# The first chunk of a streaming-encoder trunk, contraction block by contraction block: both token tiles with each block of weights, loads in that order

## The chip, the core and the metric

One NeuronCore of a Trainium2 chip runs the whole program. The metric is the device time of one execution in microseconds (us). The engines are PE (matrix multiply), ACT (activation), DVE (vector), POOL and SP; SP issues nearly all loads here, and every engine works through its own queue in the order in which the program was laid out.

## What is computed

Two layers on x of 256 tokens by 1024 features. Each layer is a half-step feed-forward block, a mixer (differential attention beside an mLSTM) and a second half-step feed-forward block, each between RMS norms:

```python
def _swiglu(h, w_in, w_out):
    gate, up = jnp.split(h @ w_in, 2, axis=-1)
    return (jax.nn.silu(gate) * up) @ w_out

for l in range(DEPTH):
    g = norm_gains[l]
    h = _swiglu(_rmsnorm(x, g[0]), ffn_w_in[l, 0], ffn_w_out[l, 0])
    x = x + 0.5 * _rmsnorm(h, g[1])
    ...
```

Only the first feed-forward block of the first layer matters here: h @ w_in for the first 256 of 2816 hidden columns (its "chunk 0"), and what comes right behind it. The contraction runs over 1024 features, in 8 blocks of 128.

## The kernel before

All large operands are split into a high and a low part, so one product of a token block with a weight block is three matmuls of 512 columns on PE: high x high, low x high, high x low. Weights come in "pieces" of 1 MB (128 x 2048), each with four contraction blocks of 512 columns (256 gate, 256 up) in the input product. A piece is loaded by SP into one of three buffers `wr`; ACT makes its high part `wh` (a cast), DVE its low part `wl` (a subtraction, the split), for the whole pieces in two halves of 1024 columns (lines 287, 288). A buffer is free for the load of the third piece behind it when DVE has split its second half. SP issues loads in order and waits for that.

The first two pieces are handled by hand (`first_chunk`, line 332). They are loaded block by block, and the table `FIRST` lists every step, in an order that all three engines keep:

- `T t hf k`: PE transposes block k of half hf of token tile t of x into a PSUM bank (line 348)
- `A`, `B` (same indices): ACT and DVE make the high and the low part of it, scaled by the gain (lines 354, 357), both into the tile `both`
- `H i k`, `L i k`: cast (ACT, 366) and split (DVE, 370) of block k of piece i
- `M t i k`: the three matmuls of tile t with block k of piece i into the tile's bank `pins[t]` (376 to 378)
- `W n`, `V n`: n filler matmuls of 512 and 128 columns on constants (`warm`, line 389), while PE has nothing to do

`start` (line 303) issues the loads of x, of the two hand-made pieces and, through `constants`, of the identity and gains `c`. Tile 0's x comes in quarters of 256 columns for the first half, otherwise in halves of 512.

What follows the first chunk is laid out by a scheduler from its own estimate of times: four squares for the norm, two for each token tile (line 438, on ACT), the input products of chunk 1 (lines 400 to 402 into `pin`, with the first two whole pieces), the hidden values h of chunk 0 (`sil` on ACT, line 265; `h` on DVE), their transposes on PE, `hh` and `hl` from these (ACT line 545, DVE line 546), and then chunk 0's output product into four banks `bk`, with `hh`, `hl` and the third whole piece. The pieces of chunk 2, the fourth and fifth, are cast and split in between. In the names of the rows `wr`, `wh`, `wl` are the pieces' tiles, c and x the constants and x, `ptr`, `pin` and `bk` PSUM banks.

Of the kernel before, what the change touches and what calls it, by code (L numbers as in the profile page):

```python
# [24 lines left out]
P = 128  # L25
# [11 lines left out]
TURN = 2  # L37
AHEAD = 2
AT = (0, 2, 6, 6, 7, 22, 24, 24, 24, 24, 36, 40, 24, 46, 34, 50, 43, 52, 52, 57, 61, 60, 61, 67, 67, 69, 71, 78, 74, 74, 78, 84)
FIRST = """W6 V3 T000 T001 A000 A001 B000 B001 W1 V1 T002 T003 H00 L00 A002 A003 B002 B003 W1 V1 M000 H01 L01  # L40
    T100 T101 T102 T103 M001 H02 L02 A100 A101 B100 B101 A102 A103 B102 B103 M002 H03 L03
    T010 T011 T012 T013 M100 A010 A011 B010 B011 A012 A013 B012 B013 T110 T111 T112 T113 M101 M102 M003 M103
    H10 L10 A110 A111 B110 B111 H11 L11 A112 A113 B112 B113 M010 M110 M011 M111 H12 L12 M012 M112 H13 L13 M013 M113"""
SCRATCH = 1024
FILL = 896
# [85 lines left out]
class _Trunk:  # L131
# [173 lines left out]
    def start(self):  # L305

        nc, a = self.nc, self.a
        sp, act = nc.sync, nc.scalar

        def load_x(q, t, hf, c=slice(0, 512)):  # L310
            q.dma_start(self.x[t][:, hf * 512 + c.start:hf * 512 + c.stop], a["x"][t, hf][:, c])

        def load_w(q, i, k, n=1):
            if k == 0:
                self.early[i] = self.raw_tile(i)
            q.dma_start(self.early[i].rearrange("p a b -> p (a b)")[:, k * 512:(k + n) * 512].rearrange("p (k c) -> p k c", k=n),
                        a["w"][i].rearrange("a b -> (a b)").rearrange("(k p c) -> p k c", k=4, p=P)[:, k:k + n])

        self.constants()
        load_x(sp, 0, 0, slice(0, 256))  # L320
        load_x(sp, 0, 0, slice(256, 512))
        load_w(act, 0, 0)
        load_w(sp, 0, 1)
        load_x(sp, 1, 0)
        load_w(sp, 0, 2)
        load_w(sp, 0, 3)
        load_x(sp, 0, 1)
        load_x(sp, 1, 1)
        load_w(sp, 1, 0, 2)
        load_w(sp, 1, 2, 2)  # L330

    def first_chunk(self, pins, xT):


        nc = self.nc
        ptr, th, tl, hi, lo = {}, {}, {}, {}, {}

        def T(t, hf, k):

            if k % 2 == 0:  # L340
                bank = (self.bank_pin if hf else self.bank_bk)((P, 4, P)) if k else self.bank_tr((P, 4, P))
                for j in range(k, k + 2):
                    ptr[t, hf, j] = bank[:, j, :]
            if k == 0:
                th[t, hf], tl[t, hf] = self.operand(hf, t, t == 0)
                xT[t].append((th[t, hf], tl[t, hf]))
            at = (4 * hf + k) * P
            nc.tensor.transpose(ptr[t, hf, k], self.x[t][:, at:at + P], self.ident)

        def gain(hf, k):  # L350
            return self.gpre[:, 4 * hf + k:4 * hf + k + 1]

        def A(t, hf, k):
            nc.scalar.activation(th[t, hf][:, k], ptr[t, hf, k], AF.Copy, scale=gain(hf, k))

        def B(t, hf, k):
            nc.vector.scalar_tensor_tensor(tl[t, hf][:, k], ptr[t, hf, k], gain(hf, k), th[t, hf][:, k].bitcast(F32),
                                           op0=ALU.mult, op1=ALU.subtract)

        def raw(i, k):  # L360
            return self.early[i].rearrange("p a b -> p (a b)")[:, k * 512:(k + 1) * 512]

        def H(i, k):
            if k % 2 == 0:
                lo[i, k // 2], hi[i, k // 2] = self.half_tiles(i, k // 2)
            self.cast = nc.scalar.activation(self.cols({k // 2: (hi[i, k // 2], lo[i, k // 2])}, k)[0], raw(i, k), AF.Copy)

        def L(i, k):
            wh, wl = self.cols({k // 2: (hi[i, k // 2], lo[i, k // 2])}, k)
            self.split = nc.vector.tensor_tensor(wl, raw(i, k), wh.bitcast(F32), op=ALU.subtract)  # L370

        def M(t, i, k):
            wh, wl = self.cols({k // 2: (hi[i, k // 2], lo[i, k // 2])}, k)
            xh, xl = th[t, i][:, k], tl[t, i][:, k]
            start, stop = (i, k) == (0, 0), (i, k) == (1, 3)
            nc.tensor.matmul(pins[t], xh, wh, start=start, stop=False)
            nc.tensor.matmul(pins[t], xl, wh, start=False, stop=False)
            nc.tensor.matmul(pins[t], xh, wl, start=False, stop=stop)  # L378

        ops = dict(T=T, A=A, B=B, H=H, L=L, M=M, W=self.warm, V=lambda n: self.warm(n, P))  # L380
        for step in FIRST.split():
            ops[step[0]](*(int(c) for c in step[1:]))

    def warm(self, n, cols=512):

        bank = self.bank_bk()
        one = self.nc.const_aps.tensor(1.0, (P, 1), mybir.dt.bfloat16)
        for _ in range(n):
            self.nc.tensor.matmul(bank[:, 0:cols], one.broadcast_to([P, P]), one.broadcast_to([P, cols]), start=True, stop=True)

    @staticmethod
    def cols(piece, k):
# [5 lines left out]
    def mm3(self, ps, xh, xl, wh, wl, start, stop):  # L398
        mm = self.nc.tensor.matmul
        mm(ps, xh, wh, start=start, stop=False)  # L400
        mm(ps, xh, wl, start=False, stop=False)  # L401
        mm(ps, xl, wh, start=False, stop=stop)  # L402
# [852 lines left out]
```

## Time and profile before

| | us |
|---|---|
| median of 3 runs | 977.52 |
| lowest, highest | 977.37, 977.88 |
| the profiled execution | 978.05 |
| its span | 976.3 |
| PE busy | 968.3 |
| DVE busy | 710.5 |
| ACT busy | 567.5 |

The profile is one execution; its times count from the span's start. A matmul's end is modelled, so PE's work is best read from the starts of its instructions. The rows of a timeline give start, duration, engine, line, output and inputs, and how often a row repeats; in brackets how long the engine was idle ahead of it and what it waited for. A DMA's row on SP or ACT (SPq, ACTq) is its issue; when its data landed stands in the view of the DMA issues.

### The profile page before, as it was taken

To read this page: it belongs to the slowest core of one execution; us is meant where nothing else is said; L and a number is where in the kernel's file an instruction comes from. 1 tells how busy PE (TensorE), PEld (TensorE's weight loads), DVE (VectorE), ACT (ScalarE), POOL (GpSimd) and SP (SyncE) were. 2 spreads that over 40 slices of the span, in tenths; PEclk is the share of its full clock that TensorE was granted. 3 is DMA by queue.
4 is the path that set the end of the run, shared out by engine and by line. 5 is a ranking of instruction groups with operands and counts; after the bars stand their busy time and mean duration, and the time that the engine had idled before them with its cause. 6 is when DMAs were issued, how large, how long until landed. Compare 5 with 4: busy or idle time off the path is not lost.

```text
span 976.3 us, 13528 instructions
## 1 busy us (share of the span) xinstructions
PE 968.3 (99%) x5067; PEld 817.2 (84%) x5067; DVE 710.5 (73%) x1177; ACT 567.5 (58%) x1041; POOL 29.0 (3%) x55
## 2 busy tenths in 40 slices
PE   9999999999999999999999999999999999999997
PEld 6888888888788888888888888888888888888886
DVE  6787676689867677667687767676997687776764
ACT  7665555477856565455475545454778475555541
POOL 2000000000010000000000000000001000000000
PEclk9999999999999999999999999999999999999999
DMA  8864545336352844564356455443454256644511
GB/s 305 335 224 167 198 170 205 134 130 232 115 193 95 315 170 175 186 238 177 133 203 241 149 206 216 175 170 116 171 211 173 87 208 239 215 176 177 198 61 44
DMA packets 27648, 178.94 MB, mean 183 GB/s; under 512 B 3034, under 2 KB 4186, under 8 KB 6846
## 3 DMA queue, kind: packets, MB, share of 16 engines
q1 hardware_dynamic: 27006, 177.46, 49.5%
q8 instruction: 40, 0.66, 0.3%
q10 hardware_dynamic: 576, 0.61, 0.2%
q14 instruction: 26, 0.21, 0.1%
HBM read 177.01 MB, written 1.05 MB: 182 GB/s over the span
## 4 chain that ended last, share of the span: by engine, by line
PE 99%; DMA 1%; DVE 0%; SPq 0%; ACT 0%; POOLq 0%; issue 0%; DVEq 0%; ACTq 0%
PE ptr L610 14%; PE pin L610 14%; PE bk L402 10%; PE bk L401 10%; PE bk L400 10%; PE pin L400 7%; PE pin L402 7%; PE pin L401 7%; PE ptr L613 7%; PE pin L613 7%; PE ptr L877 1%; PE ptr L426 1%; PE bk L1092 1%; PE bk L1130 1%; DMA x<-in_x_dram 1%; PE bk L378 0%
## 5 line engine op out<-in xcount | busy, mean ns | idle before, releaser
L288 DVE TENSOR_TENSOR wl<-wr,wh 128x1024 fp32r<-128x1024 f32 x324 | 388.6, 1222 | 127.2 <-ACT wh L287 125.2
L287 ACT ACTIVATE wh<-wr 128x1024 fp32r<-128x1024 f32 x324 | 332.2, 1053 | 121.1 <-PE ptr L610 55.9
L610 PE MATMUL pin<-both,wh 128*128 128x512 f32 x576 | 157.3, 394 | 0.0
L610 PE MATMUL ptr<-both,wh 128*128 128x512 f32 x576 | 157.0, 394 | 0.0
L401 PE MATMUL bk<-wl,hh 128*128 128x512 f32 x352 | 137.6, 391 | 0.0
L400 PE MATMUL bk<-wh,hh 128*128 128x512 f32 x352 | 137.4, 390 | 0.0
L402 PE MATMUL bk<-wh,hl 128*128 128x512 f32 x352 | 136.8, 391 | 0.0
L400 PE MATMUL pin<-wh,both 128*128 128x512 f32 x304 | 122.4, 404 | 0.0
L401 PE MATMUL pin<-wl,both 128*128 128x512 f32 x304 | 119.1, 392 | 0.0
L402 PE MATMUL pin<-wh,both 128*128 128x512 f32 x304 | 118.8, 391 | 0.0
L610 PEld LDWEIGHTS pin<-both,wh 128*128 128x128 f32 x576 | 100.6, 189 | 14.9
L610 PEld LDWEIGHTS ptr<-both,wh 128*128 128x128 f32 x576 | 98.8, 189 | 13.8
L613 PEld LDWEIGHTS ptr<-both,wl 128*128 128x128 f32 x576 | 88.3, 189 | 12.2
L613 PEld LDWEIGHTS pin<-both,wl 128*128 128x128 f32 x576 | 88.2, 189 | 11.7
L613 PE MATMUL pin<-both,wl 128*128 128x256 f32 x576 | 92.4, 281 | 0.0
L613 PE MATMUL ptr<-both,wl 128*128 128x256 f32 x576 | 91.6, 281 | 0.0
L545 ACT ACTIVATE hh<-su 128x256 fp32r<-128x256 f32 (+1 forms) x96 | 32.1, 355 | 95.4 <-PE bk L401 79.1
L402 PEld LDWEIGHTS bk<-wh,hl 128*128 128x128 f32 x352 | 66.1, 188 | 14.0
L401 PEld LDWEIGHTS bk<-wl,hh 128*128 128x128 f32 x352 | 66.1, 188 | 12.9
L400 PEld LDWEIGHTS bk<-wh,hh 128*128 128x128 f32 x352 | 66.1, 188 | 12.8
L402 PEld LDWEIGHTS pin<-wh,both 128*128 128x128 f32 x304 | 57.1, 188 | 12.4
L400 PEld LDWEIGHTS pin<-wh,both 128*128 128x128 f32 x304 | 57.2, 188 | 11.8 <-issue 0.7
(202 smaller groups left out, 978.4 us busy)
## 6 DMA issues: line engine op xcount, KB each, us to landing
wr<-in_w_dram SPq DMA_DIRECT2D x162, 1024.0 KB, 4.8
gpost<-in_gpost_dram SPq DMA_DIRECT2D x6, 512.0 KB, 5.7
wr<-in_w_dram SPq DMA_DIRECT2D x2, 512.0 KB, 6.9
wr<-in_w_dram SPq DMA_DIRECT2D x3, 256.0 KB, 5.1
x<-in_x_dram SPq DMA_DIRECT2D x3, 256.0 KB, 5.7
out_dram<-x SPq DMA_DIRECT2D x2, 256.0 KB, 2.4
x<-in_x_dram SPq DMA_DIRECT2D x2, 128.0 KB, 2.8
wr<-in_w_dram ACTq DMA_DIRECT2D x1, 256.0 KB, 3.7
```

Source lines behind the costliest of these rows:

```text
L287: ia = nc.scalar.activation(hi, raw[:, j], AF.Copy)
L288: iv = nc.vector.tensor_tensor(lo, raw[:, j], hi.bitcast(F32), op=ALU.subtract)
L400: mm(ps, xh, wh, start=start, stop=False)
L401: mm(ps, xh, wl, start=False, stop=False)
L402: mm(ps, xl, wh, start=False, stop=stop)
L426: nc.tensor.transpose(ptr[:, k, :], x[:, (4 * hf + k) * P:(4 * hf + k + 1) * P], self.ident)
L545: self.nc.scalar.activation(hh, h, AF.Copy)
L610: self.nc.tensor.matmul(b, self.cols(w, k)[0][:, c], both[:, k].rearrange("p i t -> p (i t)"), start=kh == 0 and k == 0, stop=False, skip_ ...
L613: self.nc.tensor.matmul(b[:, 0:NT * P], self.cols(w, k)[1][:, c], both[:, k, 0:NT].rearrange("p i t -> p (i t)"), start=False, stop=kh == ...
L877: self.T(ptr[:, b, :], a[:, b * P:(b + 1) * P], self.tr.ident)
L1092: self.mm(pcs[c][:, h, :], self.qkT[0][rows, h0 + h, t * P:(t + 1) * P], self.qkT[1][rows, h0 + h, 0:nk], start=True, stop=True)
L1130: self.mm(po[:, h, :], self.aT[t][:, kt, h, :], self.vd[:, kt, h * P:(h + 1) * P], start=kt == 0, stop=kt == t)
```

## The change

`FIRST` and the list of loads in `start` are written in another order, two of the fillers are left out, and all fillers write into `pins[1]`, the bank of tile 1, which tile 1's first matmul overwrites, in place of banks of their own. In the table, tile 1's first two blocks are transposed before tile 0's next two, and each block of piece 0 is used for tile 0 and then for tile 1; before, tile 0 had its first three blocks before tile 1 had one. In the loads, the first block of weights moves from ACT's queue to SP's, tile 1's first half comes in two quarters, and the first half of piece 1 in two blocks.

```diff
-FIRST = """W6 V3 T000 T001 A000 A001 B000 B001 W1 V1 T002 T003 H00 L00 A002 A003 B002 B003 W1 V1 M000 H01 L01
...
+FIRST = """W6 V3 T000 T001 A000 B000 H00 L00 W1 V1 T100 T101 A100 B100 M000 A001 B001 H01 L01 T002 T003 A101 B101 M100
...
         load_x(sp, 0, 0, slice(0, 256))
+        load_w(sp, 0, 0)
+        load_x(sp, 1, 0, slice(0, 256))
+        load_w(sp, 0, 1)
         load_x(sp, 0, 0, slice(256, 512))
-        load_w(act, 0, 0)
-        load_w(sp, 0, 1)
-        load_x(sp, 1, 0)
+        load_x(sp, 1, 0, slice(256, 512))
         load_w(sp, 0, 2)
         load_w(sp, 0, 3)
         load_x(sp, 0, 1)
+        load_w(sp, 1, 0)
         load_x(sp, 1, 1)
-        load_w(sp, 1, 0, 2)
+        load_w(sp, 1, 1)
         load_w(sp, 1, 2, 2)
...
     def first_chunk(self, pins, xT):
...
+        self.spare = pins[1]
...
     def warm(self, n, cols=512):
 
-        bank = self.bank_bk()
         one = self.nc.const_aps.tensor(1.0, (P, 1), mybir.dt.bfloat16)
         for _ in range(n):
-            self.nc.tensor.matmul(bank[:, 0:cols], one.broadcast_to([P, P]), one.broadcast_to([P, cols]), start=True, stop=True)
+            self.nc.tensor.matmul(self.spare[:, 0:cols], one.broadcast_to([P, P]), one.broadcast_to([P, cols]), start=True, stop=True)
```

On PE, the first block of tile 0 and what stands behind it, before (x_93 is x of tile 0, x_94 of tile 1, bk_113 and bk_114 are the tiles' banks):

```order
L376 MATMUL bk_113<-wh_0_144,both_129 128x512
L377 MATMUL bk_113<-wh_0_144,both_129 128x512
L378 MATMUL bk_113<-wl_0_143,both_129 128x512
L348 MATMUL ptr_160<-c_95,x_94 128x128 x2
L348 MATMUL bk_163<-c_95,x_94 128x128 x2
```

and with the change (bk_115 and bk_116 are the tiles' banks now):

```order
L351 MATMUL ptr_140<-c_95,x_94 128x128 x2
L379 MATMUL bk_115<-wh_0_135,both_129 128x512
L380 MATMUL bk_115<-wh_0_135,both_129 128x512
L381 MATMUL bk_115<-wl_0_134,both_129 128x512
L351 MATMUL bk_152<-c_95,x_93 128x128 x2
L379 MATMUL bk_116<-wh_0_135,both_129 128x512
L380 MATMUL bk_116<-wh_0_135,both_129 128x512
L381 MATMUL bk_116<-wl_0_134,both_129 128x512
L351 MATMUL bk_160<-c_95,x_94 128x128 x2
```

Tile 1's first two transposes stand ahead of the first block, tile 0's second pair behind it, and tile 1's first block comes next.

The scheduler lays out what follows in another order, too, until the third or fourth chunk. On ACT, the casts of the fourth and fifth whole piece and `hh` of chunk 0 (hh_292 for tile 0, hh_303 for tile 1), before:

```order
L287 ACTIVATE wh_0_440<-wr_437 128x1024
L287 ACTIVATE wh_1_444<-wr_437 128x1024
L545 ACTIVATE hh_292<-ptr_289 128x256
L287 ACTIVATE wh_0_450<-wr_447 128x1024
L287 ACTIVATE wh_1_454<-wr_447 128x1024
L545 ACTIVATE hh_303<-ptr_300 128x256
```

and with the change, where the same tiles are called wr_431, wr_441, hh_286 and hh_297:

```order
L287 ACTIVATE wh_0_434<-wr_431 128x1024
L287 ACTIVATE wh_1_438<-wr_431 128x1024
L287 ACTIVATE wh_0_444<-wr_441 128x1024
L287 ACTIVATE wh_1_448<-wr_441 128x1024
L547 ACTIVATE hh_286<-ptr_283 128x256
L265 ACTIVATE sil_381<-pin_331,rs_17_268 128x256
L547 ACTIVATE hh_297<-ptr_294 128x256
```

Tile 0's `hh` moves from ahead of the fifth piece's casts to behind them.

On PE, the first matmuls that read `hh`, before:

```order
L400 MATMUL bk_409<-wh_0_330,hh_292 128x512
L401 MATMUL bk_409<-wl_0_329,hh_292 128x512
L400 MATMUL bk_410<-wh_0_330,hh_292 128x512
L401 MATMUL bk_410<-wl_0_329,hh_292 128x512
L402 MATMUL bk_409<-wh_0_330,hl_293 128x512
```

and with the change:

```order
L402 MATMUL bk_403<-wh_0_324,hh_286 128x512
L403 MATMUL bk_403<-wl_0_323,hh_286 128x512
L402 MATMUL bk_404<-wh_0_324,hh_286 128x512
L403 MATMUL bk_404<-wl_0_323,hh_286 128x512
L402 MATMUL bk_405<-wh_0_324,hh_297 128x512
```

Their place is the same, behind 48 matmuls of chunk 1 and four transposes of h, and tile 1's `hh` is read earlier than before.

## Rows read from the trace of the kernel before

**Rows 1.** The chain of waits of the page, shares of the span by engine.

```profile
PE 99%; DMA 1%; DVE 0%; SPq 0%; ACT 0%; POOLq 0%; issue 0%; DVEq 0%; ACTq 0%
```

**Rows 2.** Windows: length, busy us per engine (instructions), granted clock, DMA share, GB/s.

```profile
20.00:976.00 956.00, 950.01 (x4989) 804.56 (x4987) 698.59 (x1148) 552.15 (x1005) 23.54 (x37) 1.00 0.49 180
```

**Rows 3.** Timeline of PE, 0 to 31 us.

```profile
0.76 3.04 PE L389 MATMUL bk<-const-bfloat16-1.0 128*128 128x512 bf16 x9 [0.76 <-PEq L1245]
...
6.28 0.50 PE L378 MATMUL bk<-wl,both 128*128 128x512 f32 x1
7.32 0.44 PE L348 MATMUL ptr<-c,x 128*128 128x128 f32 x2 [0.55 <-DMA x<-in_x_dram]
...
10.82 0.38 PE L348 MATMUL ptr<-c,x 128*128 128x128 f32 x2
11.04 0.38 PE L348 MATMUL pin<-c,x 128*128 128x128 f32 x2
...
11.96 0.40 PE L376 MATMUL bk<-wh,both 128*128 128x512 f32 x1
...
19.47 0.62 PE L400 MATMUL pin<-wh,both 128*128 128x512 f32 x2
...
30.89 0.39 PE L400 MATMUL bk<-wh,hh 128*128 128x512 f32 x1
```

**Rows 4.** SP's issues, then the same DMAs: KB each, us to landing.

```profile
1.17 0.42 SPq L311 DMA_DIRECT2D x<-in_x_dram  x1
1.64 0.42 SPq L316 DMA_DIRECT2D wr<-in_w_dram  x1
2.11 0.43 SPq L311 DMA_DIRECT2D x<-in_x_dram  x1
...
wr<-in_w_dram SPq DMA_DIRECT2D x1, 256.0 KB, 4.9
x<-in_x_dram SPq DMA_DIRECT2D x1, 128.0 KB, 3.2
...
x<-in_x_dram SPq DMA_DIRECT2D x1, 256.0 KB, 5.2
```

**Rows 5.** Timeline of ACT, 4 to 32 us.

```profile
4.87 0.63 ACT L366 ACTIVATE wh<-wr 128x512 fp32r<-128x512 f32 x1
...
11.69 0.61 ACT L354 ACTIVATE both<-ptr,c 128x128 fp32r<-128x128 f32 x2
...
14.25 0.64 ACT L438 ACTIVATE junk<-x 128x512 bf16<-128x512 f32 x1
...
16.70 2.01 ACT L287 ACTIVATE wh<-wr 128x1024 fp32r<-128x1024 f32 x2
...
19.43 2.00 ACT L287 ACTIVATE wh<-wr 128x1024 fp32r<-128x1024 f32 x2
21.32 0.47 ACT L265 ACTIVATE sil<-bk,rs 128x256 f32<-128x256 f32 x1
...
28.98 2.01 ACT L287 ACTIVATE wh<-wr 128x1024 fp32r<-128x1024 f32 x2
30.89 0.36 ACT L545 ACTIVATE hh<-ptr 128x256 fp32r<-128x256 f32 x1
```

**Rows 6.** DMA issues from 5.3 to 7 us: the first whole piece.

```profile
wr<-in_w_dram SPq DMA_DIRECT2D x1, 1024.0 KB, 8.3
```

**Rows 7.** Timeline of DVE: the split of the second whole piece.

```profile
20.51 2.36 DVE L288 TENSOR_TENSOR wl<-wr,wh 128x1024 fp32r<-128x1024 f32 x2
```

**Rows 8.** SP's issue of the fifth whole piece; landing of the fifth, third, sixth.

```profile
22.90 0.33 SPq L281 DMA_DIRECT2D wr<-in_w_dram  x1
...
wr<-in_w_dram SPq DMA_DIRECT2D x1, 1024.0 KB, 6.0
...
wr<-in_w_dram SPq DMA_DIRECT2D x1, 1024.0 KB, 4.8
...
wr<-in_w_dram SPq DMA_DIRECT2D x1, 1024.0 KB, 7.5
```

More of the change, by code (lines that the diff above doesn't have):

```diff
@@ L39 @@
 AT = (0, 2, 6, 6, 7, 22, 24, 24, 24, 24, 36, 40, 24, 46, 34, 50, 43, 52, 52, 57, 61, 60, 61, 67, 67, 69, 71, 78, 74, 74, 78, 84)
-FIRST = """W6 V3 T000 T001 A000 A001 B000 B001 W1 V1 T002 T003 H00 L00 A002 A003 B002 B003 W1 V1 M000 H01 L01
-    T100 T101 T102 T103 M001 H02 L02 A100 A101 B100 B101 A102 A103 B102 B103 M002 H03 L03
-    T010 T011 T012 T013 M100 A010 A011 B010 B011 A012 A013 B012 B013 T110 T111 T112 T113 M101 M102 M003 M103
+FIRST = """W6 V3 T000 T001 A000 B000 H00 L00 W1 V1 T100 T101 A100 B100 M000 A001 B001 H01 L01 T002 T003 A101 B101 M100
+    T102 T103 A002 B002 A102 B102 M001 M101 H02 L02 A003 B003 A103 B103 M002 H03 L03
+    T010 T011 T012 T013 M102 A010 A011 B010 B011 A012 A013 B012 B013 M003 T110 T111 T112 T113 M103
     H10 L10 A110 A111 B110 B111 H11 L11 A112 A113 B112 B113 M010 M110 M011 M111 H12 L12 M012 M112 H13 L13 M013 M113"""
```

## The prediction, made before the changed kernel ran

> **What bounds the kernel now.** I read the chain of waits first: it lies on PE for 99% of the span and on a DMA for 1% [rows 1]. The windows say where that 1% is: from 20 us to the end PE is busy for 950.0 of 956.0 us at full granted clock [rows 2]. So nothing behind 20 us can become shorter; only the opening has waits to give. PE's timeline prices it [rows 3]: from 11.96 to 19.47 us lie 33 matmuls of 512 columns without a gap, 0.2276 us each; two transposes take 0.22 (10.82 to 11.04), 0.11 each. The chunk has 48 such matmuls and 16 transposes, 10.92 + 1.76 = 12.7 us. It ends at 19.47, and the first nine fillers end at 3.8, so some 3.0 us are waiting, the longest visible one for x of token tile 1, until 7.32. That is the most that this change could ever win, and 0.2% of the kernel, about the least that a measurement can tell from no change, is 1.95 us.
>
> I call the loads x0a, x0b (token tile 0, columns 0-255, 256-511), x1a, x1b (token tile 1), and w00 to w03 (blocks of piece 0).
>
> **The order of loads.** Before, w01 is issued at 1.64 and lands 4.9 later, at 6.54, when 856 KB have landed; x of tile 1 is issued at 2.11 and lands 5.2 later, at 7.31, at 1112 KB [rows 4]. x0b lands at 1.17 + 3.2 = 4.37, second on SP. The new order has w00 at 472 KB, x1a at 600, w01 at 856, x0b at 984 and x1b at 1112. So x1a comes between 4.37 (x0b's old place) and 6.54 (w01), and x0b between 4.37 and about 6.9 (halfway from 6.54 to 7.31). I take about 5.2 and 6.7: the loads ahead of them are the old ones, but SP alone issues them.
>
> w00 leaves ACT's queue, where it was there for the cast at 4.87 [rows 5]. Now it is second on SP: by x0b's old place at 4.4, by the straight line through SP's two later landings (0.77 us per 256 KB) at 5.4. I take 4.87, which lies between. The Trainium skill, "DMA: Bandwidth & Descriptors" (Rules for kernel authors), says that spreading DMAs over issuing engines brings no bandwidth, only issue time. By that rule the move to SP costs w00 nothing, and the sum below stays as it is; by the line it costs 0.5 us.
>
> **PE's opening, step by step.** Before, the third matmul of the first block starts 1.41 us after the cast of w00 (4.87 to 6.28) [rows 3, 5], so with w00 at 4.87 that block ends at 6.6. Behind it in PE's queue stand the transposes of x0b, and behind those the first matmuls of tile 1: PE goes on at 6.7, when x0b lands. From there 15 blocks of three matmuls are left, 45 x 0.2276 = 10.24, 12 transposes, 12 x 0.11 = 1.36, and two or three short waits for a cast or a split, which I put at 0.25: 18.55 against 19.47, **0.9 us won**. The bounds: x0b at 6.6 or before gives 1.0; w00 at 5.4 makes the first block end at 7.1 and gives 0.5. The two fillers that go cost nothing, since PE waits there either way; that the others write to tile 1's bank adds no wait, since the same engine writes both.
>
> **SP.** Thirteen early issues stand where ten stood (w00 also left ACT). SP waits for the DMA eight issues back before it goes on, so the first whole piece is issued when x1b lands, at 7.3 at the latest, instead of 6.56. It took 8.3 us before [rows 6], to 14.86; 0.8 us later is 15.6, and ACT does not come to it before 16.1 (below): hidden, with half a microsecond of cover; without cover it would cost what it is late.
>
> **ACT, and the wait that I expect.** ACT has the same work with other neighbours. Its last seven of the chunk, from tile 1's transposes to the last cast, took 2.56 us (11.69 to 14.25) [rows 5]. Now six blocks (4.10), eight transposes (0.88) and the 0.25 stand before those transposes from 6.7 on: they begin at 11.9, ACT goes on at 12.4, 0.7 later than before, and is free at 14.95. Four squares took 2.45 us (14.25 to 16.70); now two (1.22) stand there, then two casts of 1.89 (19.43 to 21.32), then the other two squares. The second piece's casts start at 14.95 + 1.22 + 1.89 + 1.22 = 19.3, before at 19.43. So **ACT is back at its old time** at 19.3, while PE is 0.9 us ahead of its old time.
>
> What follows hangs on hh, the operand made from chunk 0's hidden values. PE needs it first for the out-product, 11.42 us behind the chunk's end (19.47 to 30.89, 48 matmuls and 4 transposes [rows 3]); the new order has as many there, so PE arrives at 18.55 + 11.42 = 29.97. Before, ACT made hh between the casts of the fourth and fifth whole piece, at 28.5, well ahead. Now it stands behind the casts of the fifth piece, which takes the buffer of the second. That buffer is free at the end of the second piece's split (22.87 before [rows 7]; 0.1 earlier now), its load was issued at 22.90 and took 6.0 us [rows 8]: the casts started at 28.98, and 1.91 us later, at 30.89, ACT was free, and made hh in 0.36 [rows 5]. So now: issue 22.8, landed 28.8, cast 28.85 to 30.75, hh until 31.1, PE goes on at 31.15. It **waits 1.2 us**, with the rest of the kernel queued behind it on PE, and stands 0.26 us later than before (30.89). The front's 0.9 us is gone.
>
> The size that I can't know is that load's duration. Whole pieces near it took 4.8 and 7.5 us [rows 8]. With 4.8 PE hardly waits: 29.97 against 30.89, 0.9 won. With 7.5 PE goes on at 32.65, 1.8 lost. I take 6.0, the same piece in the same place.
>
> Behind this PE's order differs from before until the third or fourth chunk and is then the same; hl, made after two splits, comes 0.3 us ahead of its first use, all else by 2 us or more. PE had no wait there and is now later than before, so nothing more is lost.
>
> **Sum.** 976.3 + 0.26 = 976.6 of span. The profiled execution took 978.05 with a span of 976.3 and lies 0.53 above the median 977.52; the median moves likewise, to **977.8**.
>
> **Rivals.**
> 1. *The front's gain stays.* The fifth piece lands in 4.8 to 5.1 us, as one whole piece did, and ACT has hh ready. For it speaks that the load ahead of it starts some 0.6 us earlier, since the first piece is cast and split earlier; against it that this same load took 6.0. Time 976.5 to 976.9.
> 2. *The change doesn't do what it says.* x0b lands so late (7.3) that PE's chunk ends at 19.2, and everything on ACT moves 0.6 later: hh at 31.7, 978.4.
> 3. *Slower: the load comes late.* The next load took 7.5 us; over 7.6 us the wait for hh alone reaches 1.95 us and the kernel is over 0.2% slower, 979.5 and more. It decides at the landing of the fifth piece: later than 28.5 means slower than before, later than 30.4 means measurably so.
> 4. *Slower: PE's clock.* Nine fillers of 3456 columns in all take 3.04 us at the start [rows 3], near the 1.2 GHz level; the later 512 columns in 0.2276 us are the 2.4 GHz level. The new order drops two fillers and waits between blocks. If the clock stayed or fell low over the 24 matmuls of piece 0, each takes 512 / 1.2 = 0.427 us, 24 x 0.2 = 4.8 us in all: 981 to 982. Before, waits of about half a microsecond (the one until 7.32) didn't bring the spacing down again. The Trainium skill, "TensorE: Matmul & The Clock Gate" (HAM oscillation — how this bites in real kernels), tells of kernels that wait for a DMA at every block of the contraction and start each one throttled; that speaks against this order, and no run here shows it.
>
> **Chances.** The forecast 0.60; rival 1 0.25; rival 2 0.06; rival 3 0.05; rival 4 0.03; 0.01 for an opening that wins more than all this. Faster by over 0.2% would need x0b and the fifth piece early together and more than the bound of 1.0: 0.02. Slower by over 0.2% is rivals 3 and 4, 0.08. The rest, 0.90, lies within. The range takes rival 1's lower end, 976.5, and a fifth piece of 7.1 us or so, 979.0.
>
> **What would show it.** Right: the transposes of tile 1 at 5 to 5.6 us, the first matmul of the next chunk near 18.5, PE waiting about a microsecond for ACT's hh near 30, and 30.9 to 31.4 for the first out-product. Wrong: no PE wait near 30 (rival 1), a chunk that ends at 19 or later (rival 2), matmuls of 0.43 us between 5 and 12 us (rival 4), or a PE wait at a place that I put down as covered.

## The result and the profile after

| us | before | after |
|---|---|---|
| median | 977.41 | 978.99 |
| lowest, highest | 976.99, 979.25 | 977.09, 982.54 |
| runs | 22 | 22 |

The ratio is 1.0017, interval 1.001 to 1.0024: slower, by less than the 0.2% that I called measurable. The median lies at the very top of the range, 1.2 us above the forecast, and the runs scatter over 5.5 us where before they lay within 2.3.

The profiled execution of after is its fastest run, 977.09, with a span of 975.2. The shares of the chain of waits, which answer to [rows 1]:

```profile
PE 99%; DMA 0%; SPq 0%; DVE 0%; ACT 0%; POOLq 0%; issue 0%; DVEq 0%; ACTq 0%
```

The window behind the opening, which answers to [rows 2]:

```profile
31.40:960.00 928.60, 928.60 (x4893) 787.12 (x4892) 681.47 (x1124) 539.69 (x985) 23.28 (x35) 1.00 0.49 180
```

From 31.4 to 960 us PE is busy without a break. Whatever differs lies ahead of 31.4. PE's timeline of this run, to be read beside [rows 3]:

```profile
4.71 0.68 PE L351 MATMUL ptr<-c,x 128*128 128x128 f32 x2
...
18.32 0.62 PE L402 MATMUL pin<-wh,both 128*128 128x512 f32 x2
...
29.69 0.50 PE L402 MATMUL bk<-wh,hh 128*128 128x512 f32 x1
```

The DMA issued at 1.64 on SP, x1a, with its time to landing, beside [rows 4]:

```profile
x<-in_x_dram SPq DMA_DIRECT2D x1, 128.0 KB, 3.0
```

x1a landed at 4.64, PE had no wait for it, chunk 0 ended at 18.32, and hh was ready when PE came: the fifth piece took 4.7 us. This is rival 1 of the prediction, though 977.09 lies 0.2 above that rival's 976.5 to 976.9, and it is not what most runs do. Four more traces of the same kernel (experiments 1 and 6) show the others. The columns are read from PE's timeline: PE's idle time ahead of x1a, the first matmul of chunk 1, PE's wait for hh, the first out-product matmul, and the span:

| run, us | PE idle before x1a | chunk 0 ends | wait for hh | out-product | span |
|---|---|---|---|---|---|
| 977.09 | 0 | 18.32 | 0 | 29.69 | 975.2 |
| 978.43 | 0.83 | 18.42 | 1.14 | 31.08 | 976.6 |
| 978.58 | 1.22 | 18.96 | 0.85 | 31.33 | 976.8 |
| 979.08 | 0.57 | 18.64 | 1.64 | 31.80 | 977.3 |
| 981.04 | 1.30 | 20.43 | 1.79 | 33.74 | 979.3 |

From the first out-product matmul to the end of the span it is 945.5 us in all five (945.4 in before: 976.3 - 30.89), and from the end of chunk 0 to the out-product 11.4 to 11.5 us beside the wait. So the end of chunk 0 and the wait for hh account for every run. The run of 978.43 is nearly the forecast's own scenario. Its PE timeline, beside [rows 3]:

```profile
5.59 0.45 PE L351 MATMUL ptr<-c,x 128*128 128x128 f32 x2 [0.83 <-DMA x<-in_x_dram]
...
18.42 0.62 PE L402 MATMUL pin<-wh,both 128*128 128x512 f32 x2
31.08 0.50 PE L402 MATMUL bk<-wh,hh 128*128 128x512 f32 x1 [1.14 <-ACT hh L547]
```

Its ACT timeline, the fifth piece's casts and hh, beside [rows 5]:

```profile
28.75 2.01 ACT L287 ACTIVATE wh<-wr 128x1024 fp32r<-128x1024 f32 x2 [0.55 <-DMA wr<-in_w_dram]
30.66 0.36 ACT L547 ACTIVATE hh<-ptr 128x256 fp32r<-128x256 f32 x1
```

The load of the fifth piece, beside [rows 8]:

```profile
wr<-in_w_dram SPq DMA_DIRECT2D x1, 1024.0 KB, 6.0
```

The run of 981.04 shows a third thing. Its PE timeline around the wait for x1a; the first row is a pair of fillers, of 512 and of 128 columns (W1 and V1 of the table):

```profile
4.02 0.74 PE L391 MATMUL bk<-const-bfloat16-1.0 128*128 128x512 bf16 x2
6.05 0.69 PE L351 MATMUL ptr<-c,x 128*128 128x128 f32 x2 [1.30 <-DMA x<-in_x_dram]
...
6.97 0.63 PE L380 MATMUL bk<-wh,both 128*128 128x512 f32 x1
7.40 0.63 PE L381 MATMUL bk<-wl,both 128*128 128x512 f32 x1
...
10.04 0.39 PE L380 MATMUL bk<-wh,both 128*128 128x512 f32 x1
10.27 0.39 PE L381 MATMUL bk<-wl,both 128*128 128x512 f32 x1
...
20.43 0.62 PE L402 MATMUL pin<-wh,both 128*128 128x512 f32 x2
33.74 0.50 PE L402 MATMUL bk<-wh,hh 128*128 128x512 f32 x1 [1.79 <-ACT hh L547]
```

The windows over the first fillers and over the first part behind the wait (length, busy us per engine, granted clock, DMA share, GB/s):

```profile
0.80:3.50 2.70, 2.70 (x9) 1.05 (x10) 0.08 (x2) 1.28 (x1) 2.70 (x6) 1.00 0.56 182
6.50:10.00 3.50, 3.50 (x13) 2.71 (x12) 1.89 (x5) 1.77 (x5) 0.00 (x0) 1.00 1.02 340
```

From 6.97 to 7.40 one matmul of 512 columns takes 0.43 us, the 1.2 GHz level; from 10.04 to 10.27 it takes 0.23, the 2.4 GHz level. PE had been idle for 1.30 us just before, but the clock didn't fall there: the pair of fillers ahead of the wait takes 0.74 us, and such a pair takes 0.44 at the upper level. In before that is this row:

```profile
4.71 0.44 PE L389 MATMUL bk<-const-bfloat16-1.0 128*128 128x512 bf16 x2
```

So in the run of 981.04 PE was at the lower level, at which every trace starts, ahead of the wait and behind it, and at the upper one only from about 9.6 us on. The granted-clock column says 1.00 in both windows, the one of the first fillers included, so only the spacing gives the level away; a fall it does show (0.56 in experiment 3), and here it has none. The clock had not risen yet.

### The profile page after: what moved, and what is told of

The parts are those of the page before. It is cut to its first block, busy times and chain, and to the rows that moved or that the text cites. A ratio compares the mean times of both kernels' runs of the same rounds, so it can differ in the third digit from the quotient of the medians.

```text
span 975.2 us, 13524 instructions
## 1 busy us (share of the span) xinstructions
PE 968.3 (99%) x5065; PEld 817.1 (84%) x5065; DVE 710.5 (73%) x1177; ACT 567.3 (58%) x1041; POOL 29.8 (3%) x55
## 4 chain that ended last, share of the span: by engine, by line
PE 99%; DMA 0%; SPq 0%; DVE 0%; ACT 0%; POOLq 0%; issue 0%; DVEq 0%; ACTq 0%
PE ptr L612 14%; PE pin L612 14%; PE bk L403 10%; PE bk L404 10%; PE bk L402 10%; PE pin L402 7%; PE pin L404 7%; PE pin L403 7%; PE ptr L615 7%; PE pin L615 7%; PE ptr L879 1%; PE ptr L428 1%; PE bk L1094 1%; PE bk L1132 1%; DMA x<-in_x_dram 0%; PE bk L381 0%
```

## The experiments

Theory A: the change loses its time in the wait for hh behind the fifth piece's casts. Theory B: it loses it in the opening (late loads or a low clock). After the first four runs B was split: C, PE's lower clock behind its idle time for x1a; D, loads that come late. C pictured a clock that falls in the idle time; the rows below show a fall in one trace alone, and in the others a clock that had not risen yet.

All times are medians, with lowest and highest; the before beside a kernel ran with it on the same chip. "The second experiment" in some expectations is the second kernel of experiment 1.

**1. hh taken out of the fifth piece's way, and the reverse.** The change again:

> The changed kernel once more. Theory A (the opening wins about 1.1 us, and PE then waits for hh, which ACT makes behind the casts of the fifth whole piece, whose load takes another time in every run): median near 979.0, single runs from 977 to 982; in the trace the first matmul of the next chunk at 18.3 to 18.6 us, and the first out-product matmul at 29.7 if the fifth piece lands within 4.8 us of its issue, else at its landing + 2.4 us. Theory B (the slow runs lose their time in the opening, by loads that come late on the one queue or by a low clock of PE there): in a trace of a slow run the next chunk starts at 19.5 us or later, and PE has no wait near 30 us.

979.12 (978.37 to 982.72, 10 runs), before 977.51 (976.78 to 978.35, 32 runs). The scatter of the change is its own, and before doesn't have it.

The change with hh ahead of the fifth piece's casts on ACT (`self.hh` is a list that `ffn_hilo` fills; `after` sets an order):

```diff
             ia = nc.scalar.activation(hi, raw[:, j], AF.Copy)
+            if i == 6:
+                self.after(ia, [self.hh[0]])
```

> The changed kernel with tile 0's hh of chunk 0 held ahead of the casts of the fifth whole piece on ACT, as before the change. Theory A: about 976.3, 1.1 us under the kernel before, with runs within 1 us of each other; first out-product matmul near 29.7. Theory B: as the changed kernel, median near 979 with runs up to 982.

977.64 (976.90 to 979.22, 11 runs), ratio 1.0004, interval 0.9996 to 1.0013. So 1.5 of the 1.6 us that the change loses are gone, and with them the runs above 980: A is a main term. But the front's gain does not show, and the runs fall into two groups, six from 976.90 to 977.64 and five from 978.37 to 979.22. The profiled run is the highest. Its PE timeline:

```profile
4.02 0.74 PE L394 MATMUL bk<-const-bfloat16-1.0 128*128 128x512 bf16 x2
6.16 0.69 PE L354 MATMUL ptr<-c,x 128*128 128x128 f32 x2 [1.41 <-DMA x<-in_x_dram]
...
7.08 0.63 PE L383 MATMUL bk<-wh,both 128*128 128x512 f32 x1
...
20.75 0.62 PE L405 MATMUL pin<-wh,both 128*128 128x512 f32 x2
```

x1a landed at 6.13, PE was idle for 1.41 us, and ran at the lower level ahead of it (0.74 for the pair) and behind it: from these transposes to chunk 1 are 14.59 us, in the change's run of 978.58, which was at the upper level by then, 12.99 (5.97 to 18.96). That is 1.6 us, about the distance of the two groups (means 977.1 and 978.8).

The kernel before with hh behind the fifth piece's casts:

```diff
             ia = nc.scalar.activation(hi, raw[:, j], AF.Copy)
+            if (i, j) == (6, 1):
+                self.after(self.hh[0], [ia])
```

> The kernel before, with tile 0's hh of chunk 0 held behind the casts of the fifth whole piece; loads and first chunk as before. Theory A: PE waits for hh, the out-product starts at the landing of the fifth piece + 2.4 us, which is 31.3 for a load of 6.0 us and 32.8 for one of 7.5 us, against 30.89: 977.8 to 979.4 with runs further apart than before. Theory B: as the kernel before, 977.4.

977.55 (977.05 to 978.43, 11 runs), ratio 1.0. Theory A had put this at 977.8 or more and was wrong here: the late hh alone costs nothing with the old front, where PE comes later. Its PE timeline:

```profile
6.34 0.49 PE L381 MATMUL bk<-wl,both 128*128 128x512 f32 x1
6.73 0.44 PE L351 MATMUL ptr<-c,x 128*128 128x128 f32 x2
...
18.93 0.62 PE L403 MATMUL pin<-wh,both 128*128 128x512 f32 x2
...
30.34 0.39 PE L403 MATMUL bk<-wh,hh 128*128 128x512 f32 x1
```

No wait at 30.34: the fifth piece's casts began at 27.70 and hh at 29.62. This is also the old opening in a run near the median (977.46), and chunk 0 ends at 18.93 where the profiled run of before (978.05) had 19.47 [rows 3]. That decides more than the experiment was made for (below).

**2. The halves of the change.** The new table with the old loads, hh first:

> The new table FIRST with the old list of loads, hh held ahead of the fifth piece's casts. Tile 1's transposes now stand ahead of the first block on PE and wait for x of tile 1, which the old list lands at 7.3 us: chunk 0 ends near 20.1 against 19.47 before and 18.3 after. Theory A: 978.0, runs close together. Theory B: near 977.4, if it is the loads on one queue that scatter, since these are the old ones.

978.46 (977.73 to 980.39, 11 runs), ratio 1.0012, interval 1.0003 to 1.002. PE's timeline:

```profile
6.38 0.44 PE L352 MATMUL ptr<-c,x 128*128 128x128 f32 x2 [1.56 <-DMA x<-in_x_dram]
```

The old order brings x1 whole, after w01, and the new table wants it early. The profiled run is a low one, 977.74; the runs are in two groups again, six up to 978.46 and five from 979.35 on, so this scatter doesn't need the new loads. The new loads with the old table, hh first (run later, with experiment 5):

> The new order of loads with the old order of chunk 0 (and hh of chunk 0 ahead of the fifth whole piece's casts, as the kernel before has it anyway). The old order wants x0's second half (the third and fourth transposes) before its first block of matmuls; on one queue behind w's first two blocks and x1's first half that load landed 3.9 to 4.5 us after its issue at 2.58, at 6.5 to 7.1, where before it landed near 4. Theory C: PE is idle from about 4.7 to 6.5 or 7.1, nothing waits for x1 later, chunk 0 ends 1 to 1.5 us later than in the traces of before (18.9 and 19.5), at 20 to 21: median 978.3 to 979.2, with single runs 1.6 us above these where PE then runs at its lower clock. If loads in the order of need help by themselves, the median is at or below 977.2.

979.80 (978.30 to 981.19, 11 runs), before 977.57; ratio 1.0021, interval 1.0013 to 1.003. The old table wants x0b early, which now comes late:

```profile
4.02 0.74 PE L394 MATMUL bk<-const-bfloat16-1.0 128*128 128x512 bf16 x2
6.86 0.44 PE L354 MATMUL bk<-c,x 128*128 128x128 f32 x2 [2.10 <-DMA x<-in_x_dram]
7.13 0.44 PE L394 MATMUL bk<-const-bfloat16-1.0 128*128 128x512 bf16 x2
...
7.69 0.39 PE L383 MATMUL bk<-wh,both 128*128 128x512 f32 x1
7.92 0.40 PE L384 MATMUL bk<-wl,both 128*128 128x512 f32 x1
```

The median is 0.6 above what I expected; the profiled run, 978.73, is one of its low ones. Each half alone is slower than before, and the two together with hh first are even with it. In this trace the pair of fillers takes 0.74 us ahead of the longest idle time of all (2.10 us) and 0.44 behind it: the clock rose to the upper level while PE was idle. So the idle time alone doesn't decide.

**3. Is the upper group the clock?** hh first, and six fillers of 512 columns instead of one ahead of tile 1's transposes:

```diff
-FIRST = """W6 V3 T000 T001 A000 B000 H00 L00 W1 V1 T100 ...
+FIRST = """W6 V3 T000 T001 A000 B000 H00 L00 W6 V1 T100 ...
```

> The change with hh of chunk 0 ahead of the fifth whole piece's casts (as in the second experiment), and six 512-column filler matmuls instead of one ahead of the second token tile's first transposes. In the trace of the second experiment x1's first half landed 4.5 us after its issue (6.13), PE was idle for 1.41 us before it, and the matmuls of the next 3.5 us then stood 0.42 us apart instead of 0.23, which put the end of chunk 0 at 20.75 us; in the change's first trace the same load landed 3.0 us after its issue (4.64), PE wasn't idle and chunk 0 ended at 18.32. The second experiment's runs fall into two groups, 976.9 to 977.6 (6 runs) and 978.4 to 979.2 (5 runs). Theory C (the upper group is PE at its lower clock after that idle time, about 1.7 us): five more fillers of 0.23 us keep PE busy until 5.9, the upper group is gone, all runs 976.9 to 978.0, median about 977.2. Rival D (the upper group is loads that come late, here or later): fillers change nothing of it, a third or more of the runs above 978.3, median 977.6 or up to 1 us more where x1 would have been early.

977.54 (977.00 to 978.23, 11 runs), before 977.17. One group; nothing near 979. PE's timeline:

```profile
4.09 2.77 PE L394 MATMUL bk<-const-bfloat16-1.0 128*128 128x512 bf16 x7
6.85 0.48 PE L382 MATMUL bk<-wh,both 128*128 128x512 f32 x1
...
19.39 0.62 PE L405 MATMUL pin<-wh,both 128*128 128x512 f32 x2
```

The loads are the same (x1a landed 4.1 after its issue), so D falls: filling the idle time takes the upper group away, and in both traces of that group (the one above and the next one) PE is at the lower level. But the row of the fillers corrects C. These seven hold 3200 columns; 2.77 us is the lower level for nearly all of them, and behind them PE is at the upper one. So the clock rose near 6.7 us in a run in which PE was never kept waiting from 0.76 on. The price is that the fillers, which I had put at 0.23 us each and an end at 5.9, ran a microsecond past the landing of x1a (5.73). The median is 0.3 above what I expected and gains nothing. No filler of 512 columns there:

> As the one before, but with no 512-column filler ahead of the second tile's transposes (one of 128 columns stays): PE is free 0.23 to 0.43 us earlier and idle that much longer, with the same loads. Theory C: more or most runs fall into the upper group, median 978.3 to 979, and the trace, where its run is one of these, shows matmuls 0.42 us apart after the idle time. Rival D: times as in the second experiment, median 977.6, about half of the runs below 977.7.

977.57 (976.99 to 980.07, 11 runs), against the same runs of before. Four of eleven in the upper group; C had said more than before (five of eleven), with a median of 978.3 to 979, and the median is the one given for D. So a missing filler doesn't make the lower clock more frequent. The profiled run, 979.12, is in the upper group. Its PE timeline:

```profile
5.37 0.40 PE L383 MATMUL bk<-wh,both 128*128 128x512 f32 x1
5.76 0.50 PE L384 MATMUL bk<-wl,both 128*128 128x512 f32 x1
6.84 0.64 PE L354 MATMUL bk<-c,x 128*128 128x128 f32 x2 [0.58 <-DMA x<-in_x_dram]
...
7.71 0.63 PE L383 MATMUL bk<-wh,both 128*128 128x512 f32 x1
8.13 0.63 PE L384 MATMUL bk<-wl,both 128*128 128x512 f32 x1
```

This is the one trace in which the clock fell: two matmuls of the first block start 0.39 us apart, which is less than one takes at the lower level (0.43), and behind the wait they stand 0.42 apart (7.71 to 8.13). PE had waited twice for 0.58 us. Its window, where the granted clock shows the lower level:

```profile
6.50:10.00 3.50, 3.16 (x10) 2.57 (x11) 1.56 (x4) 2.03 (x5) 0.00 (x0) 0.56 1.04 379
```

**4. The wait for hh by itself.** The change with the six fillers, hh left where the change put it:

> The change itself with the six fillers, and with hh of chunk 0 left behind the fifth whole piece's casts. Theory C: it has no runs at the lower clock, and what it takes over the kernel with fillers and hh first is the wait for hh alone: 0.3 to 1 us, median 977.5 to 978.2, with single runs up to 979. If the hh wait isn't real, it is equal to that kernel within 0.2 us. If the scatter of the change comes from neither, its runs go on reaching 980 and above.

978.83 (977.42 to 980.10, 11 runs), against 977.54 with hh first: 1.3 us for the wait. The profiled run, 979.50:

```profile
32.29 0.50 PE L402 MATMUL bk<-wh,hh 128*128 128x512 f32 x1 [1.41 <-ACT hh L547]
```

**5. x1a earlier.** hh first, x1a on ACT's queue:

```diff
         load_x(sp, 0, 0, slice(0, 256))
+        load_x(act, 1, 0, slice(0, 256))
         load_w(sp, 0, 0)
-        load_x(sp, 1, 0, slice(0, 256))
```

> As the second experiment (hh ahead of the casts), but x1's first half is issued on ACT's queue, ahead of ACT's table load and at the same time as w's first block on SP's. Issued at 1.16 instead of 1.63, and not behind w's first block on one queue, it should land near 4.2 to 5.0. Theory C: PE's idle time before it falls to 0.4 us or less, the clock stays, chunk 0 ends near 18.4 in the trace, the front's gain of about 1 us stays in the median: 976.3 to 976.9. If the landing is set by the 16 engines' bandwidth and not by the queue, it lands at 5.5 or later, and the median stays at 977.2 to 978.

977.00 (976.32 to 978.47, 11 runs), before 977.17, ratio 0.9998, interval 0.9989 to 1.0006. The load of x1a, issued at 1.16:

```profile
x<-in_x_dram ACTq DMA_DIRECT2D x1, 128.0 KB, 3.3
```

PE's timeline:

```profile
5.20 0.50 PE L382 MATMUL bk<-wh,both 128*128 128x512 f32 x1 [0.21 <-ACT wh L372]
...
18.21 0.62 PE L405 MATMUL pin<-wh,both 128*128 128x512 f32 x2
...
30.86 0.50 PE L407 MATMUL bk<-wh,hl 128*128 128x512 f32 x1 [0.20 <-DVE hl L551]
```

The same load without hh first, so the change with one line moved:

> The change with one edit: x1's first half is issued on ACT's queue at 1.16. hh of chunk 0 stays behind the fifth whole piece's casts. With hh first, this load put the end of chunk 0 at 18.21 us and the median at 977.0; in that trace the fifth piece's casts began at 29.59, so hh behind them would be ready at 31.9 and PE, there at 29.49, would wait 2.3 us. Theory A plus C: the earlier opening is swallowed by the wait for hh, median 978.0 to 979.2, runs from 976.8 (fifth piece landed early) to 980. If the change lost its time in the opening alone, this is equal to the kernel with hh first: median 976.8 to 977.2.

978.63 (976.84 to 980.67, 11 runs), before 977.57. PE's timeline:

```profile
17.98 0.61 PE L402 MATMUL pin<-wh,both 128*128 128x512 f32 x2
31.14 0.50 PE L402 MATMUL bk<-wh,hh 128*128 128x512 f32 x1 [1.65 <-ACT hh L547]
```

The earliest end of chunk 0 of all traces, and the out-product starts no sooner than in before [rows 3]: PE is early for nothing. x1a on SP, ahead of w00, hh first:

```diff
         load_x(sp, 0, 0, slice(0, 256))
+        load_x(sp, 1, 0, slice(0, 256))
         load_w(sp, 0, 0)
-        load_x(sp, 1, 0, slice(0, 256))
```

> hh of chunk 0 first, and x1's first half issued on SP's queue ahead of w's first block instead of behind it (issues at 1.17 and 1.64, one queue). If what matters is that x1's 128 KB are not behind w's 256 KB on the queue, x1 lands 2.8 to 3.3 us after its issue, at 4.0 to 4.5, w's first block at 4.9 to 5.4; the first matmul block starts at 5.6 to 6.1 and chunk 0 ends near 18.6 to 19: median 976.9 to 977.5, no run above 978.5 unless PE's idle time there (about 0.7 us) takes the clock down. If one queue is simply slower than two, x1 lands after 5 and the median is 977.5 to 978.

978.89 (977.69 to 979.35, 11 runs), above what I expected. Now w00 is late (3.9 us after its issue at 1.64), the wait is ACT's cast of it, and PE is at the lower level behind that wait in the profiled run, 979.29 (ahead of it too: its fillers at 4.02 take 0.74):

```profile
6.21 0.80 PE L382 MATMUL bk<-wh,both 128*128 128x512 f32 x1 [1.02 <-ACT wh L372]
6.80 0.63 PE L383 MATMUL bk<-wh,both 128*128 128x512 f32 x1
7.23 0.63 PE L384 MATMUL bk<-wl,both 128*128 128x512 f32 x1
```

The wait went from one load to the other. Two queues brought both by 4.9 us in all four traces, one queue in two of the ten with x1a third on SP. Last, x1a on ACT's queue, with hh and hl also ahead of the second half of the fourth piece:

```diff
-            if i == 6:
+            if (i, j) == (5, 1) or i == 6:
                 self.after(ia, [self.hh[0]])
...
+            if (i, j) == (5, 1):
+                self.after(iv, [self.hl[0]])
```

> x1's first half on ACT's queue, and hh and hl of chunk 0 ahead not only of the fifth whole piece's casts but of the second half of the fourth's. In the trace with hh alone first, PE waited 0.20 us for hl, which stood behind both of the fourth piece's subtractions on DVE (28.11 to 30.39). Theory: that wait goes, the median is 0.1 to 0.3 lower than that kernel's, 976.7 to 976.9. Rival: the fourth piece's second half is now late for PE, or ACT's idle time is passed on to the pieces behind: equal, or up to 1 us more.

976.95 (976.64 to 977.19, 11 runs), before 977.57, ratio 0.9993, interval 0.9984 to 1.0001. Once more, in experiment 6's company:

> The last variant again (x1's first half on ACT's queue, hh and hl of chunk 0 ahead of the fourth piece's second half): if it is below the kernel before, its median is 976.7 to 977.1 once more, and no run is above 977.6, while the kernel before lies at 977.2 to 977.6.

976.86 (976.45 to 977.22, 11 runs), before 977.21 (15 runs), ratio 0.9994, interval 0.9985 to 1.0003. PE's timeline:

```profile
18.23 0.61 PE L408 MATMUL pin<-wh,both 128*128 128x512 f32 x2
29.51 0.47 PE L408 MATMUL bk<-wh,hh 128*128 128x512 f32 x1
30.52 0.39 PE L410 MATMUL bk<-wh,hl 128*128 128x512 f32 x1
```

ACT's timeline:

```profile
27.95 0.38 ACT L553 ACTIVATE hh<-ptr 128x256 fp32r<-128x256 f32 x1 [1.25 <-PE ptr L544]
```

ACT idles 1.25 us for hh, and PE has no wait left. None of its 22 runs is above 977.22, so the scatter is gone. By the medians it is 0.4 to 0.6 us below before, and both intervals still hold 1: the gain is likely, not shown.

**6. The change itself, three more traces.**

> The change, unaltered, for one more trace. In all traces so far the time from the first matmul of the out-product to the end of the span was 945.4 to 945.9 us, and the run took 1.75 to 1.85 more than its span. So the time should follow from three terms in the opening: PE's idle time ahead of x1 (1.2 to 1.6 us where x1 lands near 6), the lower clock behind it (matmuls 0.42 us apart, 1.6 us in all), and the wait for hh (0 to 1.7 us). A run above 980 must show the lower clock and the wait for hh together; a run below 978 neither.

> The same kernel again, the same three terms: the end of chunk 0 near 18.3 (x1 early), near 19 (x1 near 6, clock kept) or near 20.6 (clock lowered), then 11.4 us and the wait for hh to the first out-product, then 945.5 us to the end of the span. If a slow run shows none of these, something else makes the scatter.

> The same kernel again, the same three terms as for the two looks before it.

978.43, 979.08 and 981.04: the rows of the table above. Each is the sum of the terms, and the one above 980 has the lower clock and the wait for hh together. The lower clock behind x1a, seen until then only in variants, is in the change too. In the run of 979.08 two matmuls at most ran slow (5.67 to 6.65), and the fifth piece took 6.5 us.

## Why the prediction was wrong

Most steps held in their places:

- *x1a at 5.2, between 4.37 and 6.54.* In ten traces with x1a third on SP it landed at 4.6 to 6.1, six of them at 5.7 or later (issue at 1.63 or 1.64, 3.0 to 4.5 us). Inside the bounds; the value was about half a microsecond early. What makes it land early or late was not found.
- *w00 at 4.87, between 4.4 and 5.4.* 3.9 to 4.1 in the same ten traces, earlier than both bounds. It changed nothing, since PE never waited for its cast in the five traces of the change.
- *x0b at 6.7, by 6.9.* 6.4 to 7.1 in the five traces of the change.
- *Chunk 0 ends at 18.55.* 18.32, 18.42, 18.64 and 18.96 in four traces, 20.43 in the one with the lower clock.
- *SP's first whole piece at 7.3 at the latest, hidden.* 6.9 to 7.7, over the bound in two traces; PE has no wait for it in any. *ACT at the second piece's casts at 19.3:* 19.09 (977.09) and 19.71 (978.58), 21.20 in the run with the lower clock.
- *hh behind the fifth piece.* I had the load at 6.0 us, hh at 31.1, PE waiting 1.2 us and going on at 31.15. The run of 978.43: 6.0, 31.02 (30.66 + 0.36), 1.14, 31.08. The other waits: 0, 0.85, 1.64 and 1.79. Taking hh out of the way gave 1.3 and 1.5 us in the medians (experiments 4 and 1).
- *The span of 976.6.* 976.6 in that run.

**The step that failed is the last one of the sum**: "The profiled execution took 978.05 [...] and lies 0.53 above the median 977.52; the median moves likewise". That excess was not spread over the run. It lay in the opening, in a load that the change moves: x of tile 1. In the profiled run of before it landed 5.2 us after its issue, and its transposes start at 7.32 [rows 3, 4]; in experiment 1's run of the old opening, near the median, it landed 4.6 us after the same issue, and they start at 6.73 without a wait. The first block ahead of them was no earlier there: its third matmul starts at 6.34, against 6.28. Chunk 0 ends at 18.93 against 19.47, and the out-product begins at 30.34 against 30.89, 0.54 and 0.55 earlier. So the typical run of before had half of the front's 0.9 us already, the change won it only against a late run, and I took the excess off the result as though the change's runs shared it. That the one run near the median is typical, the second kernel of experiment 1 bears out: with hh out of the way and in its lower group, the change's front is worth 0.4 us (mean 977.1, before 977.5), which is 0.9 less 0.5. Without that step the forecast is 978.3, 0.7 from the median.

**The rest is a rival sized wrongly in both directions, and a wait a little short.** I gave the clock 3% and 4.8 us over all of piece 0. The runs show it in a part of the executions (one of five traces of the change; by the upper groups about four in ten runs of the two variants with hh first), over six or seven of the 24 matmuls of piece 0, at 1.4 to 1.6 us (14.38 us in the run of 981.04 from tile 1's transposes to chunk 1, and 14.59 in experiment 1, against 12.99). The rival said "stayed or fell low", and my reason, that waits of half a microsecond in before had not brought the spacing down, spoke against falling alone. In three of the four traces with six or more such matmuls it was staying: the fillers ahead of the wait are at the lower level already. In before the clock had risen by 4.71, so its waits could not show that. The Trainium skill, "TensorE: Matmul & The Clock Gate" (HAM oscillation — how this bites in real kernels), tells of the other half, a clock that falls while PE waits for a DMA; only the variant without the filler shows that here.

The wait for hh, 1.2 us in the sum, measured 1.3 to 1.5 by the pairs of medians. An estimate from these medians: the lower group with hh first, 977.1, and 1.3 to 1.5 of waiting give 978.4 to 978.6 for the change without the lower clock; the 0.4 to 0.6 that are left to 978.99 would be the clock in a part of the runs, and were not measured by themselves.

Rival 1 was not wrong as a mechanism: the profiled run is it. Rival 2 comes nearest in the run of 978.58: x0b landed at 7.10 (7.3 there), chunk 0 ended at 18.96 (19.2), hh was ready at 31.28 (31.7). In rival 3 a figure is read wrongly: with a fifth piece of 7.6 us the 1.9 us are what the kernel loses against before (32.75 against 30.89), while the wait for hh itself would be 2.8.

## What to carry to other kernels

Ask where a profiled run's excess over the median lies before you carry it over: if it sits in the stretch that the change touches, the gain worked out there is partly the excess. An earlier front is worth only what the next operand allows; here a whole microsecond of it ended in a wait for hh, and paid only once hh was moved ahead of casts that nobody waited for. Early in a kernel a load that PE waits for with nothing to do can cost more than the wait: in three traces PE went idle for 1.0 to 1.4 us while still at half its clock, and stayed there to 9.4 us or later. To tell a clock that fell from one that has not risen, read the spacing of the matmuls ahead of the wait as well as behind it.

## What the runs showed of the hardware

- **The second queue.** x1a on ACT's queue is issued 0.47 us earlier (1.16 against 1.63) and landed at 4.5 to 4.9 in four traces (3.3 to 3.7 us after its issue), against 4.6 to 6.1 in ten with it on SP. w00, issued on SP at the same time, then landed at 4.3 to 4.7, against 3.9 to 4.1 in the ten. The prediction cited the Trainium skill, "DMA: Bandwidth & Descriptors" (Rules for kernel authors), that spreading over issuing engines saves issue time alone. Eight of the ten landings on SP are at 5.3 or later, so x1a gained up to 1.6 us, more than the issue time, and here the measurement decides; w00 lost 0.2 to 0.8. That the second queue makes the kernel faster is not shown: the medians are 977.00 (before 977.17, interval of the ratio 0.9989 to 1.0006) with x1a on ACT's queue and 977.64 (before 977.51, 0.9996 to 1.0013) with it on SP.
- **When the clock rises differs from run to run.** PE starts at the lower level in every trace (nine fillers in 3.0 us). With the same work ahead of it, the pair of fillers at 4.02 takes 0.74 us, all at the lower level, in all five traces of the change. Behind it PE was at the upper level after 0.83 and 1.22 us of idle time (the runs of 978.43 and 978.58), after 0.57 us from 6.6 on (979.08), and after 1.30 us from 9.6 on (981.04). In the variants it was at the upper level after 1.56 and 2.10 us, and at the lower after 1.02 and 1.41. What sets the moment no row shows.
- **The granted-clock column can't be read ahead of that rise.** In the run of 981.04 it says 1.00 for 0.8 to 3.5 us, where the fillers of 512 columns run at the lower level, and for 6.5 to 10, where matmuls stand 0.43 us apart. It says 0.56 for 6.5 to 10 in the trace in which the clock had risen and fell again.
